# A decoder trunk on one core: the sum A21 + A22 of each Strassen pair made by an accumulating DMA, the other weight forms rebuilt from it, and the raw weights in four regions

## The chip, the core and the metric

The kernel runs on one NeuronCore of a Trainium2 chip. TensorE (PE in the profile) multiplies, VectorE (DVE) and ScalarE (ACT) do elementwise work, GpSimd (POOL) does a few small operations, and SyncE (SP) issues every DMA of the kernel before the change. The metric is the device time of one execution in microseconds. Three executions of the kernel before took 2245.98, 2249.03 and 2248.22 us; the median is 2248.22 us.

## The reference, cut to what matters

One decoding step of a small trunk of two layers, for 512 prompt tokens and 8 sample tokens, so 520 tokens in all, with 2048 channels:

```
for i in range(DEPTH):                                   # 2 layers
    h = rmsnorm(x, norm_g)
    z = h @ w_in                                         # [520, 2048] @ [2048, 8192]
    b_c, c_c, x_c, g_c, q, k, v, g_r = split_projection(z)
    y_conv = b_c * conv3(c_c * x_c) * silu(g_c)
    y_ret  = group_norm(retention(rope(q), rope(k), v)) * silu(g_r)
    x = x + concat(y_conv, y_ret) @ w_out                # [520, 2048] @ [2048, 2048]
    x = x + sigmoid(x @ w_pg) * (p[i] @ w_ple)           # [520, 2048] @ [2048, 2048]
y = rmsnorm(x, final_g)
```

All is float32. Nearly all arithmetic lies in the products with `w_in`, `w_out` and `w_pg`. The outputs also hold the new states of the convolution and of the retention, the latter 256 KB for each head and sample.

## The kernel before, in words

**Products.** The channels lie on the partitions. A weight matrix is cut into M tiles (128 output channels) and K tiles (128 input channels); the tokens are cut into two halves of 260. Each float32 operand is split into two float32r parts that add up exactly (`split`, `split_w`), and a product takes three matmuls of a 128x128 weight tile with 128x260 tokens (`mm3`, lines 216 to 218 of the profile): high by high, high by low, low by high.

**Strassen pairs.** Two neighbouring M tiles go together in `strassen`. Over the first `s` K tiles (a number from the tables `HEADS`, `CONVS`, `OUTS`, `GATES`, one for each pair) it forms seven products in place of eight; the weights of one pair are four blocks A11, A12, A21, A22 of `q = s // 2` K tiles each, and the products need A11, A12, A22 and the four forms A21+A22, A21+A22-A11, A11-A21, and A12 less the second of these. The other `KT - s` K tiles go by plain products at the end of the pair. The tables hold 89 Strassen pairs; 34 of them have `s = 14`, so q = 7. Over all pairs q adds up to 452.

**Weights.** `raws` (and `load`, for the plain K tiles) asks `raw_ring` for a place and issues the DMAs from SP (line 268, pieces of 2 or 3 K tiles; line 191, pieces of up to 4). The ring is 36 units of one weight tile; a request gets the neighbouring units that have been free for longest, at any start. `add` (line 275, DVE) makes the four forms in place, in pieces of up to 3 tiles. `split_w` (ACT line 198, DVE line 199) splits a piece into `split_ring`, a ring of 60 units, which holds the high and low parts of 30 tiles; the matmuls read there. A piece of `raw_ring` is free when its last split is done, and a piece of `split_ring` when its last matmul is done.

**Order.** A scheduling layer sets the order of each engine's instructions when the program is built, from priorities (weights have a raised one, `WPRIO`). The order on each engine, on each queue and on each ring is then fixed; SP, POOL, ACT and DVE wait in that order.

**Stages.** Each layer has: the retention heads (four groups of M tiles, with small matmuls for scores and states between the pairs, taken from the list `later` by `aside()`, and with the decode steps of the samples, `sample_step`, lines 579 to 587, which load a state and broadcast rows `kq` and store the new state `o_rets`); the convolution (8 groups of two pairs, mostly q = 7); the output projection; and the gate. In the profiled execution the heads run at about 50 to 450 us and 1130 to 1560 us, and the convolutions behind them.

**POOL** does only three sorts of work in the running part: a memset of `qks`, the powers -1/2 of the group norms (`rstp`, line 728) and those of the channel norms (`r5p`, line 456).

Of the kernel before, what the change touches and what calls it, by code (L numbers as in the profile page):

```python
# [13 lines left out]
P = 128  # L14
# [26 lines left out]
# How many K tiles go by Strassen in each pair of M tiles of the four products with weights.  # L41
# [13 lines left out]
def k_order(s):  # L55
    """The K tiles of a product whose first s go by Strassen: the first of each pair, the second, the rest."""
    return list(range(0, s, 2)) + list(range(1, s, 2)) + list(range(s, KT))


class Slots:  # L60
    """Equal on-chip slots of [128, 520] words, given out oldest-freed first."""
# [22 lines left out]
class Ring:  # L84
    """On-chip place for weights, in units of one tile; a request gets the neighbouring units freed longest ago."""

    def __init__(self, pool, n, dtype, name):
# [4 lines left out]

    def get(self, n):
        _, i = min((max(self.freed[i : i + n]), i) for i in range(len(self.freed) - n + 1))
# [6 lines left out]
    def fits(self, n):  # L101
        return min(max(self.freed[i : i + n]) for i in range(len(self.freed) - n + 1)) < BUSY
# [8 lines left out]
class Banks:  # L111
    """The accumulators of the products with weights, given out oldest-freed first."""
# [17 lines left out]
class Val:  # L130
    """A product's [128, 520] result: two accumulators, or a slot. Iterates as (tokens, view)."""
# [18 lines left out]
class Op:  # L150
    """A [128, 520] operand in two parts: a slot for each part, or a slot for each half of the tokens."""
# [13 lines left out]
def trunk_kernel(  # L165
# [17 lines left out]
    raw_ring = Ring(const, RAW, F32, "raw")  # L183
# [18 lines left out]
    def chunks(a, b, most=CH):  # L202
        """a to b in equal pieces: [(first, after last)]"""
# [10 lines left out]
    def mm3(out, wh, wl, xh, xl, start, stop, more=False):  # L214
        """more: the sum goes on after a stop and a read"""
# [6 lines left out]
    def product(out, w, c, xs, start, stop, more=False):  # L222
        """out (+)= sum over i of W[:, tile c + i]^T X[i], all in two parts"""
# [10 lines left out]
    def aside():  # L234
        """Work of the tensor engine that waits for a place between two products"""
        if later:
            later.pop(0)()

    def gemm(ops, src, s):
        """One M tile, all tokens; the K tiles lie in k_order(s)."""  # L240
# [10 lines left out]
    def strassen(ops, sums, src0, src1, s):  # L251
        """Two M tiles: Strassen's seven products in Winograd's form over the first s K tiles (halves of
        M, of K and of the tokens), the plain products over the others."""
# [949 lines left out]
```

## Time and profile before

| | |
|---|---|
| median of three executions | 2248.22 us |
| span of the profiled execution, first to last instruction | 2245.6 us |
| the difference of these two, which lies around the span | 2.6 us |
| DVE busy | 1837.1 us, 82% |
| ACT busy | 1290.3 us, 57% |
| POOL busy | 31.4 us, 38 instructions |
| HBM read, written | 294.70 MB, 43.58 MB |

The times of the profile come from one execution on the chip. A group's row gives the line of the source, the engine, the operation, the tiles written and read, the shapes, the count, then after the bar its busy time, the mean duration of one in ns, and the idle time of the engine just before these instructions with what ended most of it. Matmuls overlap, so their mean duration (284 ns) is longer than the time from one to the next.

### The profile page before, as it was taken

The page shows a single profiled execution, that of the slowest core. Times are in us where ns is not written, and L with a number is a line of the kernel's source. Part 1 is how long each engine was busy: PE and PEld are TensorE (multiplying, and loading weights), DVE is VectorE, ACT ScalarE, POOL GpSimd, SP SyncE. Part 2 cuts the span into 40 slices and gives each one's busy share as a digit, 9 for nine tenths or more (in the row PEclk, how much of TensorE's full clock was granted, in tenths as well). Part 3 has the DMA queues.
Part 4 walks back from the last instruction along what each step waited for, and adds up shares of the span by engine and source line. Part 5 has one row for each costly group of instructions (what it writes and reads, how often), then busy time and mean ns, then how long its engine had stood idle before and what let it go on. Part 6 is the DMA issues. An engine that isn't in the chain of part 4 may idle for free.

```text
span 2245.6 us, 50947 instructions
## 1 busy us (share of the span) xinstructions
PE 2219.0 (99%) x18364; PEld 2212.4 (99%) x18364; DVE 1837.1 (82%) x4363; ACT 1290.3 (57%) x3119; POOL 31.4 (1%) x38
## 2 busy tenths in 40 slices
PE   9999999999999999999999999999999999999998
PEld 8999999999999999999999999999999999999998
DVE  7787878788998888878786878787998888789785
ACT  6555555555655545655754455555565555556565
POOL 0000000000000000000000000000000000000000
PEclk9999999999999999999999999999999999999999
DMA  7445454644334645645743463546443345447445
GB/s 245 126 144 165 153 182 135 186 126 133 109 98 125 207 123 155 194 150 154 228 127 103 134 195 116 186 144 188 128 122 100 116 148 177 150 131 222 136 141 185
DMA packets 243582, 341.65 MB, mean 152 GB/s; under 512 B 28032, under 2 KB 153472, under 8 KB 243328
## 3 DMA queue, kind: packets, MB, share of 16 engines
q1 hardware_dynamic: 243328, 338.39, 49.0%
q8 instruction: 144, 2.36, 0.4%
q14 instruction: 110, 0.90, 0.1%
HBM read 294.70 MB, written 43.58 MB: 151 GB/s over the span
## 4 chain that ended last, share of the span: by engine, by line
PE 92%; DMA 5%; DVE 1%; ACT 1%; issue 1%; SPq 0%; DVEq 0%; POOL 0%; ACTq 0%
PE ps_g L216 28%; PE ps_g L217 28%; PE ps_g L218 28%; DMA slot<-kq 2%; DMA o_rets<-slot 1%; PE ps_p L216 1%; PE ps_p L217 1%; PE ps_p L218 1%; DMA slot<-x2s 1%; PE ps_s L216 0%; PE ps_s L218 0%; PE ps_s L217 0%; PE ps_o L218 0%; PE ps_o L217 0%; PE ps_o L216 0%
## 5 line engine op out<-in xcount | busy, mean ns | idle before, releaser
L216 PE MATMUL ps_g<-slot,split 128*128 128x260 f32 x5640 | 1577.1, 284 | 18.3 <-ACT slot L263 10.2
L217 PE MATMUL ps_g<-slot,split 128*128 128x260 f32 x5640 | 1585.7, 283 | 0.0
L218 PE MATMUL ps_g<-slot,split 128*128 128x260 f32 x5640 | 1572.4, 283 | 0.0
L198 ACT ACTIVATE split<-raw 128x256 fp32r<-128x256 f32 (+3 forms) x1738 | 797.8, 476 | 668.9 <-PE ps_g L217 341.8
L216 PEld LDWEIGHTS ps_g<-slot,split 128*128 128x128 f32 x5640 | 1057.0, 189 | 20.8 <-ACT slot L263 12.4
L217 PEld LDWEIGHTS ps_g<-slot,split 128*128 128x128 f32 x5640 | 1065.2, 189 | 0.3 <-DVE slot L377 0.2
L218 PEld LDWEIGHTS ps_g<-slot,split 128*128 128x128 f32 x5640 | 1057.5, 189 | 0.0
L199 DVE TENSOR_TENSOR split<-raw,split 128x256 fp32r<-128x256 f32 (+2 forms) x1738 | 827.6, 496 | 237.8 <-ACT split L198 121.2
L275 DVE TENSOR_TENSOR raw<-raw 128x256 f32<-128x256 f32 (+2 forms) x768 | 345.9, 465 | 10.3 <-DMA raw<-wo 3.3
L263 ACT ACTIVATE slot<-ps_g 128x260 f32<-128x260 f32 x445 | 167.8, 377 | 46.4 <-PE ps_g L218 43.3
L263 DVE TENSOR_TENSOR slot<-ps_g,slot 128x260 f32<-128x260 f32 x267 | 111.6, 421 | 18.8 <-PE ps_g L218 17.9
L376 ACT ACTIVATE slot<-slot 128x520 fp32r<-128x520 f32 (+1 forms) x189 | 104.9, 583 | 38.1 <-DVE slot L355 8.7
L377 DVE TENSOR_TENSOR slot<-slot,slot 128x520 fp32r<-128x520 f32 (+1 forms) x189 | 115.7, 631 | 5.8 <-ACT slot L376 5.3
L582 ACT ACTIVATE slot<-slot,vs 128x256 f32<-128x256 f32 x128 | 58.3, 502 | 97.8 <-DMA slot<-kq 74.5
L542 DVE TENSOR_TENSOR slot<-slot,slot 128x520 f32<-128x520 f32 x142 | 95.5, 692 | 6.1 <-PE ps_o L218 5.9
L583 DVE SCALAR_TENSOR_TENSOR slot<-slot,vec,slot 128x512 f32<-128x512 f32 x64 | 47.8, 749 | 54.3 <-ACT slot L582 47.1
L587 DVE CUSTOM_DVE_ANT_0 slot<-slot,slot 128x256 f32<-128x256 f32 x128 | 49.3, 418 | 0.1
L263 DVE TENSOR_TENSOR slot<-slot 128x260 f32<-128x260 f32 x89 | 37.5, 421 | 0.1
L216 PE MATMUL ps_p<-slot,split 128*128 128x260 f32 (+1 forms) x124 | 35.0, 282 | 0.0
L217 PE MATMUL ps_p<-slot,split 128*128 128x260 f32 (+1 forms) x124 | 34.9, 282 | 0.0
L218 PE MATMUL ps_p<-slot,split 128*128 128x260 f32 (+1 forms) x124 | 34.9, 281 | 0.0
L440 DVE TENSOR_TENSOR slot<-slot,slot 128x520 f32<-128x520 f32 x43 | 29.8, 694 | 4.4 <-ACT slot L439 4.4
(172 smaller groups left out, 1216.1 us busy)
## 6 DMA issues: line engine op xcount, KB each, us to landing
raw<-wi SPq DMA_DIRECT2D x268, 192.0 KB
raw<-wi SPq DMA_DIRECT2D x388, 128.0 KB
raw<-wi SPq DMA_DIRECT2D x117, 256.0 KB
slot<-kq SPq DMA_DIRECT2D x64, 256.0 KB
slot<-sret SPq DMA_DIRECT2D x64, 256.0 KB
o_rets<-slot SPq DMA_DIRECT2D x64, 256.0 KB
slot<-x1s SPq DMA_DIRECT2D x60, 260.0 KB
slot<-x2s SPq DMA_DIRECT2D x54, 260.0 KB
```

The costliest lines, as they stand in the source:

```text
L198: S.activation(hi, raw, AF.Copy)
L199: V.tensor_tensor(lo, raw, F(hi), SUB)
L216: PE.matmul(out, wh, xh, start=start, stop=False, skip_group_check=more)
L217: PE.matmul(out, wh, xl, start=False, stop=False, skip_group_check=more)
L218: PE.matmul(out, wl, xh, start=False, stop=stop, skip_group_check=more)
L263: fn(*args)
L275: V.tensor_tensor(out[:, n], x[:, n], y[:, n], op)
L376: S.activation(hi, src[:, n], AF.Copy)
L377: V.tensor_tensor(lo, src[:, n], F(hi), SUB)
L542: V.tensor_tensor(out[:, n], v, table[:, n], MUL)
L582: S.activation(kv[:, 256 * e : 256 * e + 256], kb[:, 256:512], AF.Identity, scale=vs[:, h, e, b : b + 1])
L587: V.tensor_tensor_reduce(kv[:, c], st[:, c], kb[:, :256], 1.0, 0.0, MUL, ADD, osum[:, e, h, b : b + 1])
```

## The change

It does four things.

1. In `strassen`, A21 is loaded by SP as before, and then POOL issues DMAs that read A22 from HBM and add it to A21 in its place (`G.dma_start(..., accum_op=ADD)`, line 300 of the new file), one for each piece of 2 or 3 K tiles. The place then holds A21 + A22. A22 is still loaded by itself as well, now asked for before the first product instead of behind it.
2. The other forms are rebuilt from it with three adds in place of four: A11 - (A21 + A22), then A11 - A21 as that plus A22, then A12 plus that first form. The first of these has the other sign than the form it replaces, and so `operand_sums` makes its second sum with the other sign; its fourth keeps its value.
3. `raw_ring` gets a step: a request of more than 4 units may start only at the units 0, 8, 16 and 24, a smaller one at every fourth unit.
4. In the products' order, the place that held A11 now carries the third and sixth product and the one that held A21 the fifth; which place is given back first changes with it.

```diff
-    def __init__(self, pool, n, dtype, name):
+    def __init__(self, pool, n, dtype, name, step=0):
+        self.step = step
...
+    def starts(self, n):
+
+        return range(0, len(self.freed) - n + 1, (self.step if n > 4 else 4) if self.step else 1)
+
     def get(self, n):
-        _, i = min((max(self.freed[i : i + n]), i) for i in range(len(self.freed) - n + 1))
+        _, i = min((max(self.freed[i : i + n]), i) for i in self.starts(n))
...
-    raw_ring = Ring(const, RAW, F32, "raw")
+    raw_ring = Ring(const, RAW, F32, "raw", 8)
...
         w11 = raws(src0, 0)
+        w21 = raws(src1, 0)
+        for i, j in chunks(0, q, CHL):
+            G.dma_start(w21[:, P * i : P * j], src1[:, P * (q + i) : P * (q + j)], accum_op=ADD)
+        w22 = raws(src1, q)
         times(a, w11, k1, True, False)
         copy(z0[:, LEFT], a)
-        w21, w22 = raws(src1, 0), raws(src1, q)
         add(w11, w11, w21, SUB)
-        add(w21, w21, w22, ADD)
         times(b, w21, t1, True, False)
         copy(z1[:, RIGHT], b)
-        add(w21, w22, w11, SUB)
-        times(a, w21, t2, False, True)
+        add(w21, w11, w22, ADD)
+        times(a, w11, t2, False, True)
         copy(z0[:, RIGHT], a)
         w12 = raws(src0, q)
-        add(w21, w12, w21, SUB)
+        add(w11, w12, w11, ADD)
         times(d, w12, at(ops, k2, LEFT), True, False)
         raw_ring.put(w12)
         aside()
-        times(a, w11, t3, False, True)
-        raw_ring.put(w11)
+        times(a, w21, t3, False, True)
+        raw_ring.put(w21)
...
-        times(b, w21, at(ops, k2, RIGHT), False, True)
-        raw_ring.put(w21)
+        times(b, w11, at(ops, k2, RIGHT), False, True)
+        raw_ring.put(w11)
...
-        V.tensor_tensor(t12[:, RIGHT], f1[:, RIGHT], t12[:, LEFT], SUB)
+        V.tensor_tensor(t12[:, RIGHT], t12[:, LEFT], f1[:, RIGHT], SUB)
         V.tensor_tensor(t34[:, LEFT], f1[:, RIGHT], f0[:, RIGHT], SUB)
-        V.tensor_tensor(t34[:, RIGHT], f1[:, LEFT], t12[:, RIGHT], SUB)
+        V.tensor_tensor(t34[:, RIGHT], f1[:, LEFT], t12[:, RIGHT], ADD)
```

The rest of the diff takes out comments, which moves line numbers: 191, 198, 199, 268 and 275 become 196, 203, 204, 273 and 280, and 456, 622 and 728 become 464, 630 and 736.

Three places show what moves. The first is POOL in the first head of layer 0, before and after (`rstp` is the power of the group norm, `raw` the raw weights, `wi` the packed `w_in`):

```order
L456 TENSOR_TENSOR r5p<-r_596,half_neg 128x5
L622 MEMSET qks 128x128
L728 TENSOR_TENSOR rstp<-rstd,half_neg 128x2 x2
L622 MEMSET qks 128x128
```

```order
L464 TENSOR_TENSOR r5p<-r_596,half_neg 128x5
L300 DMA raw<-wi 128x256
L630 MEMSET qks 128x128
L300 DMA raw<-wi 128x384
L300 DMA raw<-wi 128x256 x2
L736 TENSOR_TENSOR rstp<-rstd,half_neg 128x2 x2
L300 DMA raw<-wi 128x256 x3
```

The powers now stand in line with DMAs that wait for loads; over the program POOL gets 192 such DMAs.

The second is SP at a q = 7 pair in the middle of the convolutions of layer 0, the one whose weights are loaded from 566 us on, before and after. A block of 7 K tiles is three DMAs (2, 2 and 3 tiles), so a pair's blocks read 256, 256, 384, and the two K tiles left over are the two DMAs of line 191 (196):

```order
L268 DMA raw<-wi 128x256 x2
L268 DMA raw<-wi 128x384
L268 DMA raw<-wi 128x256 x2
L268 DMA raw<-wi 128x384
L268 DMA raw<-wi 128x256 x2
L268 DMA raw<-wi 128x384
L268 DMA raw<-wi 128x256 x2
L268 DMA raw<-wi 128x384
L191 DMA raw<-wi 128x256 x2
```

```order
L273 DMA raw<-wi 128x256
L273 DMA raw<-wi 128x384
L273 DMA raw<-wi 128x256 x2
L273 DMA raw<-wi 128x384
L273 DMA raw<-wi 128x256 x2
L273 DMA raw<-wi 128x384
L273 DMA raw<-wi 128x256 x2
L273 DMA raw<-wi 128x384
L273 DMA raw<-wi 128x256
L196 DMA raw<-wi 128x256 x2
```

Before, the blocks come as A11, A21, A22, A12. After, the second and third piece of A12 come first, then A11, A21, A22, and A12's first piece last, since a leftover K tile of the pair ahead lies in that piece's units; each piece of A21 is issued two DMAs later.

The third is DVE at the same pair, before and after (line 199/204 the split, 275/280 the adds, 263/268 the sums of results):

```order
L275 TENSOR_TENSOR raw<-raw 128x256 x4
L199 TENSOR_TENSOR split<-raw,split 128x384
L275 TENSOR_TENSOR raw<-raw 128x384
L199 TENSOR_TENSOR split<-raw,split 128x256
L275 TENSOR_TENSOR raw<-raw 128x384
L199 TENSOR_TENSOR split<-raw,split 128x256
L275 TENSOR_TENSOR raw<-raw 128x256
L263 TENSOR_TENSOR slot_447_7546<-slot_447_7546 128x260
```

```order
L280 TENSOR_TENSOR raw<-raw 128x256
L204 TENSOR_TENSOR split<-raw,split 128x256
L280 TENSOR_TENSOR raw<-raw 128x256
L204 TENSOR_TENSOR split<-raw,split 128x384
L280 TENSOR_TENSOR raw<-raw 128x384
L204 TENSOR_TENSOR split<-raw,split 128x256 x2
L280 TENSOR_TENSOR raw<-raw 128x256
L268 TENSOR_TENSOR slot_447_7546<-slot_447_7546 128x260
```

Before, the first six adds make A11 - A21 and A21 + A22; after, the first three make A11 less the sum that the DMAs have made, and the three of the sum are gone.

More of the change, by code (lines that the diff above doesn't have):

```diff
@@ L101, in fits @@
     def fits(self, n):
-        return min(max(self.freed[i : i + n]) for i in range(len(self.freed) - n + 1)) < BUSY
+        return min(max(self.freed[i : i + n]) for i in self.starts(n)) < BUSY
     def put(self, *parts):
```

## The prediction

> **What bounds the kernel now.** I read the page's first part, then its groups, then PE's idle time, then the stretches of the program.
>
> ```profile
> PE 2219.0 (99%) x18364; PEld 2212.4 (99%) x18364; DVE 1837.1 (82%) x4363; ACT 1290.3 (57%) x3119; POOL 31.4 (1%) x38
> L216 PE MATMUL ps_g<-slot,split 128*128 128x260 f32 x5640 | 1577.1, 284 | 18.3 <-ACT slot L263 10.2
> L198 ACT ACTIVATE split<-raw 128x256 fp32r<-128x256 f32 (+3 forms) x1738 | 797.8, 476 | 668.9 <-PE ps_g L217 341.8
> L275 DVE TENSOR_TENSOR raw<-raw 128x256 f32<-128x256 f32 (+2 forms) x768 | 345.9, 465 | 10.3 <-DMA raw<-wo 3.3
> ```
>
> PE is busy for 2219.0 us of a span of 2245.6 us: 18364 matmuls at 2219.0 / 18364 = 0.121 us from one to the next. The change adds and drops no matmul, so all that it could save is the 26.6 us in which PE is idle. Of these the row of line 216 names 18.3 us of waits. ACT's row says the same from the other side: the splits wait for PE to free their ring (341.8 us behind line 217 alone), so weights are normally ready ahead of need. The next view, waits of PE, tells what the 18.3 us are:
>
> ```profile
> PE ps_g L216 <- ACT slot L263: 10.2, 8, 2.4
> PE ps_g L216 <- ACT slot L379: 5.5, 1, 5.5
> PE ps_g L216 <- ACT split L198: 1.5, 1, 1.5
> ```
>
> 5.5 us is the start, before any weight; the change does not touch it. 10.2 us in 8 waits is PE waiting for ACT to copy an accumulator. Only 1.5 us is a late split. Sums by stretch (length; busy PE, PEld, DVE, ACT, POOL; clock; DMA share; GB/s) show where:
>
> ```profile
> 50.00:450.00 400.00, 396.33 (x3270) 393.91 (x3270) 316.57 (x805) 216.53 (x534) 7.25 (x12) 1.00 0.50 155
> 450.00:750.00 300.00, 300.00 (x2507) 300.00 (x2506) 258.17 (x637) 172.10 (x443) 5.43 (x1) 1.00 0.42 125
> 1130.00:1560.00 430.00, 420.32 (x3425) 417.37 (x3426) 338.34 (x834) 230.10 (x552) 8.43 (x11) 0.99 0.47 144
> 1560.00:1860.00 300.00, 300.00 (x2509) 300.00 (x2508) 264.80 (x642) 174.61 (x435) 5.87 (x1) 1.00 0.43 129
> ```
>
> The convolutions (second and fourth row), where most pairs have q = 7 and DVE is fullest (258 of 300 us), have no idle PE at all. The heads (first and third) have 3.7 and 9.7 us. The chain of waits just ahead of the longest of these stops, and of one more, reads (start, us, what):
>
> ```profile
> 1226.45 5.23 DMA o_retp<-slot
> ...
> 1231.74 4.16 DMA slot<-kq
> ...
> 1235.93 0.91 ACT slot L582 x2
> 1236.83 0.28 ACT slot L263
> ```
> ```profile
> 1432.07 6.07 DMA slot<-kq
> ...
> 1441.38 5.47 DMA o_rets<-slot
> ```
>
> A decode step's DMA of 256 KB takes 4 to 6 us, ACT stands at it in order (line 582), and the copy that PE needs (line 263) stands behind. So the kernel is PE-bound throughout, and its few stops come from DMA latency through ACT, not from DVE.
>
> **The change, part by part. DVE's adds.** Three adds stay of four, so 768 / 4 = 192 go. At the group's mean that is 192 x 0.465 = 89 us of DVE, 4% of the span. In the convolutions it can save nothing: PE has no idle there. In the heads it shortens the way to a kq load only where that load stands behind a DVE split in SP's queue. I take -1 us, with bounds of 0 and -9: half of the 18.3 us, since the other half is the start's 5.5 us and the landings themselves.
>
> **The accumulating DMAs.** 192 of them read the 452 K tiles of A22 once more: 452 x 64 KiB = 29.6 MB on top of 341.65 MB moved. They lengthen one chain: load of A21, POOL, accumulate, split, product. No row shows an accumulating DMA, and none a DMA issued by POOL. Nearest rows, of the chain of waits and of two tiles on POOL:
>
> ```profile
> 431.74 3.01 DMA slot<-xT
> ```
> ```profile
> 328.29 3.60 DMA raw<-wi
> 1115.51 5.24 DMA raw<-wi
> ```
> ```profile
> L728 POOL TENSOR_TENSOR rstp<-rstd,half_neg x16: 695/698/1070, 110.3 to 1533.8; 128x2 f32<-128x2 f32 x16
> ```
> ```profile
> L456 POOL TENSOR_TENSOR r5p<-r,half_neg x3: 850/1177/1957, 44.0 to 2226.1; 128x5 f32<-128x5 f32 x2, 128x3 f32<-128x3 f32 x1
> ```
>
> Lower bound: the shortest plain transfer, 3.0 us, issue included. Upper bound: POOL's slowest small operation and two of the slowest transfers one after the other, since the sum's place has to be read and written back: 2.0 + 2 x 6.07 = 14.1 us. I take a middling POOL operation and a usual load, 1.2 + 3.6 = 4.8 us, the value nearest to the rows of the same tile.
>
> Does 4.8 us fit? Take the pair that the order shows. A21's first piece is issued where A22's was, two DMAs later, so at the 570.66 below; the split of the finished sum stood at 579.00:
>
> ```profile
> 570.66 0.33 SPq L268 DMA_DIRECT2D raw<-wi  x1
> ```
> ```profile
> 579.00 0.42 ACT L198 ACTIVATE split<-raw 128x256 fp32r<-128x256 f32 x1 [0.57 <-PE ps_g L217]
> ```
>
> That is 8.3 us; less a load of 3.6 us, 4.7 us are left. So at 4.8 us the sum is just in time for the same split, which itself waited for PE ("<-PE ps_g L217") and so was not late. Behind it stands the stock: 60 units hold 30 tiles in two parts, 30 x 3 x 0.121 = 10.9 us of matmuls at most. Counted along the waits of the changed order, 119 matmuls stand between the one whose end lets that load go and the first that cannot run without its sum: 119 x 0.121 = 14.4 us. Off that go a split on DVE (0.42), SP's issue (0.33), a load (3.6) and ACT's split and copy (0.42 + 0.38): 9.2 us are left for an accumulate. The tightest chains of all, in the heads, have 80 and 83 matmuls (9.7 and 10.0 us), which leave 4.5 and 4.9 us. Cost at 4.8 us: 0.3 us. The cover is this stock; without it, each us over 9.2 costs a us in each of 34 pairs.
>
> [...]
>
> **The engines that move the data.** The queue row and the waits of SP's queue:
>
> ```profile
> q1 hardware_dynamic: 243328, 338.39, 49.0%
> ```
> ```profile
> SPq L268 <- DVE split L199: 576.2, 380, 10.5
> SPq L580 <- PE ps_o L217: 15.9, 6, 3.3
> ```
>
> 338.39 MB take 49.0% of 16 engines; 29.6 MB, counted twice because the place is read too, is 59 / 338 x 49 = 8.6 points more. I take 5% longer landings, 0.25 us on 5 us, for the 8 waits of the heads: +2 us, with bounds of 0 and +12 (1.5 us on each of 8).
>
> **Four regions.** A q = 7 block used to take exactly 7 units anywhere; now it starts at 0, 8, 16 or 24, and a leftover piece of 1 to 3 tiles closes a whole region until it is split. Loads that go later: in the order of before, past the start, none has fewer than 16 us between the matmul that frees its place and the one that needs its own product; after, 17 have, the two least of them, at about 1367 and 1465 us, 6.2 and 7.9 us (matmuls times 0.121). A plain load needs 0.42 + 0.33 + 3.6 + 0.42 + 0.42 = 5.2 us of that with the DVE split. With a landing of 5.24 us it is 6.8, and both are in the heads, where ACT also stands at kq loads. SP waits for a place most of its time (576.2 us in 380 waits), so a late place holds back what is queued behind it, kq loads (line 580) included. I take +2 us, bounds 0 and +8 (2 us at each of the four least).
>
> **POOL's queue.** The powers (16 of `rstp`, 0.70 us each) now stand behind accumulating DMAs that wait for loads. Behind `rstp` come ACT's normalisation, the transposes of the gate and, in SP's queue, `o_retp` and a kq load, as in the chain at 1226 us. Counted along the waits, the matmuls between what `rstp` needs and what needs it stay 6.5 us or more as before; a POOL issue of 1 us ahead of it fits. Cost 0, bounds 0 and +4 (one us at four of them).
>
> **Signs of the token sums, changed order of the places.** Same instructions, same shapes: 0.
>
> The sum: 2245.6 - 1 + 0.3 + 2 + 2 = 2248.9 us of span; with the 2.6 us that lie around it, 2251.5 us against 2248.22: I predict **2251 us**.
>
> **The rivals.**
>
> *Faster through DVE.* If the kq stops were partly DVE's (the split that SP waits for comes later even when DVE is 78% busy), 89 us less of it would halve PE's 18.3 us: 2248.22 - 9 = 2239; with the +2 of the regions 2241 us. For it: SP's 576.2 us behind DVE splits. Against it: chains ahead of the stops are DMA for 4 to 6 us each, DVE for less than 1.
>
> *Slower through a long accumulate.* One mechanism: the piece of A21 becomes a sum later than the stock lasts, in each q = 7 pair. It decides from 9.2 us on; at 10.5 us it costs 34 x 1.3 = 44 us: 2295 us; at the upper bound 34 x 4.9 = 167 us. For it: nothing in the trace shows such a DMA. Against it: no single transfer in the chain takes over 6.07 us.
>
> *Slower through slower landings.* If an accumulate keeps the engines busy several times longer than a plain load of its size, every landing grows by 1.5 us: +12 us on the heads' 8 waits and as much again where loads with little time come late: 2248 + 24 less what DVE gives, some 2270 us. For it: 4 to 6 us landings at a share of 0.47 to 0.50. Against it: at the start, at a share of 0.81, PE is idle 5.5 of 50 us, which is its wait for the first operand and nothing else.
>
> ```profile
> 0.00:50.00 50.00, 44.47 (x343) 43.99 (x344) 36.02 (x69) 37.81 (x81) 2.07 (x10) 1.00 0.81 269
> ```
>
> *POOL shut out by DVE.* If POOL could prepare a DMA only while DVE rests (42 of 300 us in the first convolutions), one us of preparation would take 300 / 42 = 7 us, the accumulate 3.6 + 8.2 = 11.8 us: 34 x 2.6 = +88 us, 2340 us. [...] I give it little.
>
> **How the numbers follow.** Chances: forecast 0.55 (2244 to 2258), faster through DVE 0.18, slower landings 0.15, long accumulate 0.08, POOL shut out 0.04. A measurement of this kernel tells a change of about 0.2%, 4.5 us, from none: under 2243.7 is faster, over 2252.7 slower. Faster: 0.15 of the DVE case and 0.02 of the forecast, 0.17. Slower: 0.27 of the three slow cases and 0.12 of the forecast's upper part, 0.39. Same: 0.44. The range 2242 to 2275 leaves out half of the DVE case (0.09) and the two slowest cases (0.12).
>
> **What would show it.** PE busy within 3 us of 2219.0 and no idle PE in the convolutions show that the accumulate is covered; idle PE there in every pair, behind line 203, shows the long accumulate. DVE near 1750 us with PE's waits on ACT's line 268 unchanged at 8 to 14 us shows that DVE was not the limit; waits halved show the first rival. Landings of kq in the chain at 4 to 6 us show that the engines cope; 6 to 8 us the slower landings. A row on POOL for line 300 of over 2 us, or some rows far longer than others, shows POOL shut out. New waits of PE for a split near 1367 or 1465 us show the regions. I am wrong if the accumulate holds the ring's places so long that SP's queue stops as a whole, which no row here prices.

## The result, and the profile after

| | before | after |
|---|---|---|
| median of four executions | 2247.1 us | 2338.59 us (2326.15 to 2339.94) |
| ratio, 95% interval | | 1.040 (1.038 to 1.0419) |
| span of the profiled execution | 2245.6 us | 2335.5 us |
| PE busy, PE idle in the span | 2219.0 us, 26.6 us | 2248.4 us, 87.1 us |

The changed kernel is 4% slower, some 90 us, where 2251 us and at most 2275 us had been predicted. The span grew by 89.9 us: 60.5 us are idle PE, 29.4 us more busy PE. The page's first part and its groups, of the changed kernel:

```profile
PE 2248.4 (96%) x18364; PEld 2230.6 (96%) x18364; DVE 1750.3 (75%) x4171; ACT 1266.8 (54%) x3119; POOL 201.4 (9%) x230
L221 PE MATMUL ps_g<-slot,split 128*128 128x260 f32 x5640 | 1596.0, 286 | 78.5 <-ACT slot L268 70.1
L203 ACT ACTIVATE split<-raw 128x256 fp32r<-128x256 f32 (+3 forms) x1738 | 777.5, 474 | 705.0 <-PE ps_g L222 257.8
L280 DVE TENSOR_TENSOR raw<-raw 128x256 f32<-128x256 f32 (+2 forms) x576 | 262.9, 468 | 207.2 <-DMA raw<-wi 132.1
```

DVE became 87 us shorter, as the adds that went away promised, and nothing came of it. DVE now stands idle for 207.2 us ahead of the adds that remain (line 280), where the group of before had 10.3 us. PE's waits for ACT to copy an accumulator (line 268) went from 10.2 to 70.1 us. The waits, by engine and line (us in total, times, longest), tell what ACT and DVE wait for:

```profile
PE ps_g L221 <- ACT slot L268: 70.1, 44, 4.3
DVE raw L280 <- DMA raw<-wi: 132.1, 62, 5.7
DVE raw L280 <- DMA raw<-wo: 47.7, 18, 5.6
DVE raw L280 <- DMA raw<-wg: 23.3, 11, 4.3
ACT split L203 <- DMA raw<-wi: 107.0, 54, 7.0
ACT split L203 <- DVE raw L280: 95.9, 66, 6.8
ACT slot L590 <- DMA slot<-kq: 79.5, 41, 4.7
```

The kq waits of the decode steps hardly moved (74.5 us before), and ACT's waits for DVE's adds fell (132.3 us before). What grew are the waits of DVE's add and of ACT's split for a transfer of weights: before, ACT's split waited 6.5 us in all for `wi`, and DVE's adds 3.3 us for `wo`. Sums by stretch, of the changed kernel (heads and convolutions of layer 0, its projection and gate, then the same of layer 1):

```profile
50.00:450.00 400.00, 392.05 (x3205) 389.21 (x3205) 301.68 (x765) 212.67 (x520) 29.41 (x38) 0.99 0.56 162
450.00:850.00 400.00, 394.00 (x3263) 391.56 (x3263) 311.37 (x755) 211.47 (x554) 45.51 (x47) 1.00 0.55 147
850.00:1150.00 300.00, 287.33 (x2339) 285.19 (x2339) 225.16 (x506) 175.73 (x420) 19.98 (x23) 0.98 0.59 171
1150.00:1580.00 430.00, 418.38 (x3380) 414.39 (x3379) 317.55 (x775) 223.90 (x538) 35.95 (x40) 0.98 0.53 154
1580.00:1880.00 300.00, 282.08 (x2314) 279.03 (x2313) 229.34 (x565) 156.94 (x404) 31.65 (x37) 0.99 0.51 136
1880.00:2335.00 455.00, 429.98 (x3525) 427.16 (x3524) 328.30 (x738) 248.32 (x605) 35.78 (x36) 0.98 0.57 168
```

and of the kernel before, the two stretches of projections and gates, which the prediction did not show:

```profile
850.00:1130.00 280.00, 279.46 (x2330) 279.03 (x2328) 232.03 (x517) 177.90 (x414) 0.00 (x0) 1.00 0.57 177
1860.00:2245.00 385.00, 378.42 (x3158) 378.12 (x3156) 306.94 (x679) 226.16 (x541) 2.33 (x3) 0.99 0.52 162
```

Length less PE's busy time is idle PE. The heads had 13.4 us (3.7 + 9.7) and now have 19.6; the convolutions had none and have 23.9 (6.0 + 17.9); projections and gates had 7.1 (0.5 + 6.6) and have 37.7 (12.7 + 25.0). So the cost is not in the convolutions alone, and least in the heads, where PE already waited.

**One late sum, step by step.** The timeline of the changed kernel at the pair that the prediction used, start and duration of each group of instructions (in brackets the idle time ahead of it and what ended it):

```profile
576.98 0.37 ACT L268 ACTIVATE slot<-ps_g 128x260 f32<-128x260 f32 x1
580.42 0.20 ACT L818 ACTIVATE ncv<-slot 128x2 f32<-128x2 f32 x1 [3.07 <-DVE slot L550]
...
581.25 1.12 ACT L203 ACTIVATE split<-raw 128x256 fp32r<-128x256 f32 x3
...
582.19 0.89 DVE L204 TENSOR_TENSOR split<-raw,split 128x256 fp32r<-128x256 f32 x2
...
584.40 0.86 POOL L300 DMA_DIRECT2D raw<-wi  x1 [18.60 <-DMA raw<-wi]
585.66 1.75 POOL L300 DMA_DIRECT2D raw<-wi  x2 [0.40 <-issue]
...
588.86 0.43 DVE L280 TENSOR_TENSOR raw<-raw 128x256 f32<-128x256 f32 x1 [2.23 <-DMA raw<-wi]
...
591.32 0.43 DVE L280 TENSOR_TENSOR raw<-raw 128x256 f32<-128x256 f32 x1 [1.70 <-DMA raw<-wi]
...
591.33 0.42 ACT L203 ACTIVATE split<-raw 128x256 fp32r<-128x256 f32 x1 [2.04 <-DMA raw<-wi]
591.65 0.37 ACT L268 ACTIVATE slot<-ps_g 128x260 f32<-128x260 f32 x1
...
592.07 0.39 PE L221 MATMUL ps_g<-slot,split 128*128 128x260 f32 x1 [1.14 <-ACT slot L268]
```

Follow the second piece of A21. The matmul that lets its place be emptied ends at 577.5. But ACT stands in order at line 818, the convolution's elementwise work, and waits there 3.07 us for DVE; so the split that empties the place starts on ACT at 581.25 and on DVE at 582.19. SP issues the load at 582.63, it lands at 585.13; POOL's accumulate is issued at 585.66 and lands at 591.22. 13.7 us have gone by since the matmul. In the same 0.1 us DVE's add and ACT's split start, which had waited for it; ACT's copy of an accumulator stands behind that split, and PE, which waits for that copy, starts 0.4 us after it has started, having been idle for 1.14 us. PE does not wait for a weight, then: it waits for a copy that is queued behind a split that waits for a sum. DVE itself was behind at that time: it had waited 3.3 us in all for three sums of the pair ahead (stops that ended at 567.17, 569.40 and 570.89 us), and then worked without a pause until 581.2 us.

**The busy time.** Part of the 29.4 us more of busy PE is a lower clock. In the trace's clock records the granted clock falls to 0.5 in 12 stretches ahead of the end (3 before), 10 of 3.41 us and 2 of 6.83 us. Two pieces beside each other in the changed kernel, behind a stop of 3.09 us that ended at 965.0:

```profile
966.00:969.00 3.00, 3.00 (x15) 3.00 (x15) 3.00 (x7) 1.81 (x3) 0.00 (x0) 0.50 0.38 112
969.00:972.00 3.00, 3.00 (x27) 3.00 (x26) 2.09 (x5) 0.81 (x3) 0.00 (x0) 0.99 0.47 138
```

15 matmuls in 3 us against 27. From one matmul's start to the next, 382 intervals in the run lie between 0.20 and 0.26 us, 199 more than before; at 0.10 us more than the usual 0.12 each, that is 20 us. Most of the rest of the busy time is the last matmul of each stop, which shows at its full 0.28 us: start-to-start gaps of over 0.4 us were 15, and are 60.

### The profile page after: what moved, and what is told of

The parts are those of the page before. It is cut to its first block, busy times and chain, and to the rows that moved or that the text cites. A ratio compares the mean times of both kernels' runs of the same rounds, so it can differ in the third digit from the quotient of the medians.

```text
span 2335.5 us, 51521 instructions
## 1 busy us (share of the span) xinstructions
PE 2248.4 (96%) x18364; PEld 2230.6 (96%) x18364; DVE 1750.3 (75%) x4171; ACT 1266.8 (54%) x3119; POOL 201.4 (9%) x230
## 3 DMA queue, kind: packets, MB, share of 16 engines
q0 software_dynamic: 27648, 29.63, 8.3%
## 5 line engine op out<-in xcount | busy, mean ns | idle before, releaser
L221 PE MATMUL ps_g<-slot,split 128*128 128x260 f32 x5640 | 1596.0, 286 | 78.5 <-ACT slot L268 70.1
L203 ACT ACTIVATE split<-raw 128x256 fp32r<-128x256 f32 (+3 forms) x1738 | 777.5, 474 | 705.0 <-PE ps_g L222 257.8
L204 DVE TENSOR_TENSOR split<-raw,split 128x256 fp32r<-128x256 f32 (+2 forms) x1738 | 816.8, 498 | 211.5 <-ACT split L203 135.1
L280 DVE TENSOR_TENSOR raw<-raw 128x256 f32<-128x256 f32 (+2 forms) x576 | 262.9, 468 | 207.2 <-DMA raw<-wi 132.1
L300 POOL DMA_DIRECT2D raw<-wi x132 | 115.5, 943 | 1215.6 <-DMA raw<-wi 872.7
L385 DVE TENSOR_TENSOR slot<-slot,slot 128x520 fp32r<-128x520 f32 (+1 forms) x189 | 116.5, 635 | 10.3 <-ACT slot L384 10.2
L550 DVE TENSOR_TENSOR slot<-slot,slot 128x520 f32<-128x520 f32 x142 | 95.9, 694 | 6.1 <-PE ps_o L223 5.8
L300 POOL DMA_DIRECT2D raw<-wo x32 | 28.0, 982 | 289.8 <-DMA raw<-wo 245.2
L300 POOL DMA_DIRECT2D raw<-wg x28 | 24.3, 897 | 332.9 <-DMA raw<-wg 213.4
L268 DVE TENSOR_TENSOR slot<-slot 128x260 f32<-128x260 f32 x89 | 37.7, 423 | 2.8 <-ACT slot L268 2.8
L576 ACT ACTIVATE slot<-slot 128x520 f32<-128x520 f32 x32 | 20.2, 634 | 30.2 <-DVE slot L550 30.2
```

Source lines behind the costliest of these rows:

```text
L203: S.activation(hi, raw, AF.Copy)
L204: V.tensor_tensor(lo, raw, F(hi), SUB)
L221: PE.matmul(out, wh, xh, start=start, stop=False, skip_group_check=more)
L268: fn(*args)
L280: V.tensor_tensor(out[:, n], x[:, n], y[:, n], op)
L300: G.dma_start(w21[:, P * i : P * j], src1[:, P * (q + i) : P * (q + j)], accum_op=ADD)
```

## The experiments

Two theories go through the expectations. **L**: the sum is late. Its chain (a matmul frees the place, split, load, accumulate, then add and split in the order of DVE and ACT) is longer than the matmuls that stand beside it. **R**: the rest of the change does it, the four regions above all. Every time below is a median beside the kernel before on the same chip, every ratio is to that kernel, with its 95% interval.

### Which part of the change costs

`no_pool` and `pool_plain` edit the accumulating DMA:

```diff
-        for i, j in chunks(0, q, CHL):
-            G.dma_start(w21[...], src1[...], accum_op=ADD)      # no_pool
...
-            G.dma_start(w21[...], src1[...], accum_op=ADD)      # pool_plain
+            G.dma_start(w21[...], src1[...])
```

`dve_sum` is no_pool with one add more, and `regions_only` is the kernel before with the two lines of the ring:

```diff
+        add(w21, w21, w22, ADD)                                 # dve_sum, behind copy(z0[:, LEFT], a)
...
-    raw_ring = Ring(const, RAW, F32, "raw")                     # regions_only, with the class Ring of after
+    raw_ring = Ring(const, RAW, F32, "raw", 8)
```

> The changed kernel without its 192 accumulating DMAs: A21 stands where A21 + A22 should, which part of the computation is left out; the four regions, the three adds and the order of requests stay. Theory L (the loop: a place freed by a DVE split, load of A21, accumulate, the add on DVE that waits for it in order; DVE idles about 4 us in each q = 7 pair): the stops of PE go, 2245 us +- 6, PE's waits on ACT's copy back at 8 to 14 us, and clock at 0.5 in 3 to 5 stretches. Theory R (the regions give places late): stays over 2300. Theory T (more bytes keep the DMA engines busy, all landings later): also 2245, so this run does not tell L from T.

> The same 192 DMAs from POOL behind the load of A21, but plain: A22 overwrites A21, so A21 is left out of the sum. Theory L (it is the second transfer in line that costs, whatever it does): 2315 to 2345 us, POOL DMA to landing 3.5 to 4.5 us in place of 4.9. Theory C (adding in the DMA engines is what costs): landing under 3 us and under 2280 us.

> The kernel before with the four regions alone; adds, forms and request order of before. Theory R: over 2300 us. Theory L: the regions cost what late places cost by themselves, 2247 to 2260 us, no stop of PE in the q = 7 stretches.

> The changed kernel with the sum A21 + A22 made by a fourth add on DVE, no DMA from POOL; regions, forms and early request of A22 stay. Theory L: 2245 to 2262 us: all but the accumulate is harmless. Theory R: over 2300 us. A time over 2262 with DVE above 81% would say that the order of requests costs as well.

| | time | ratio |
|---|---|---|
| no_pool | 2247.79 us | 1.0008 (0.9993 to 1.0022) |
| pool_plain | 2275.07 us | 1.0142 (1.0109 to 1.0174) |
| regions_only | 2249.67 us | 1.0011 (0.9999 to 1.0023) |
| dve_sum | 2251.99 us | 1.0024 (1.0012 to 1.0037) |

Without the accumulating DMAs all other parts of the change together cost nothing that can be measured, and less work for DVE brings nothing: no_pool has both the regions and 1771.6 us of DVE, 66 us less than before. R falls. By the first line of its page PE is as busy as before:

```profile
PE 2214.7 (99%) x18364; PEld 2207.3 (98%) x18364; DVE 1771.6 (79%) x4171; ACT 1289.2 (57%) x3119; POOL 34.4 (2%) x38
```

A second transfer in line, even a plain one, costs 1.4%, some 32 us; that it accumulates costs 2.6% more, some 58 us. Neither expectation for pool_plain came true: L had 2315 us or more, and C, whose time it is (under 2280 us), had a landing under 3 us. What differs between these two is told by POOL's and the queue's rows, here of pool_plain:

```profile
L300 POOL DMA_DIRECT2D raw<-wi x132: 536/536/719, 44.8 to 1845.7; - x132
q0 software_dynamic: 10304, 29.63, 4.2%
raw<-wi POOLq DMA_DIRECT2D x86, 128.0 KB, 3.3
raw<-wi POOLq DMA_DIRECT2D x46, 192.0 KB, 3.9
```

and here of the changed kernel (min/median/max ns of one; packets, MB, share of 16 engines; KB and median us from issue to landing):

```profile
L300 POOL DMA_DIRECT2D raw<-wi x132: 862/865/1538, 44.7 to 1896.4; - x132
q0 software_dynamic: 27648, 29.63, 8.3%
raw<-wi POOLq DMA_DIRECT2D x86, 128.0 KB, 4.8
raw<-wi POOLq DMA_DIRECT2D x46, 192.0 KB, 5.1
```

For the same 29.63 MB an accumulate takes 0.33 us more of POOL, 2.7 times the packets, twice the engines' time and, in these rows of `wi`, 1.2 to 1.5 us more from issue to landing. Whether the 58 us come from the longer chain or from the doubled traffic these runs did not tell.

### Traffic or lateness

`acc_aside` keeps the traffic and takes it out of the chain; `spare` is a tile of four units that nobody reads, and a small POOL operation that reads two words of A21 makes each accumulate wait for the load of A21 as before:

```diff
+            o = 2 * P * (i == 2 and j == 4)
+            G.tensor_tensor(spare[:, o : o + 2], w21[:, P * i : P * i + 2], w21[:, P * i : P * i + 2], ADD)
-            G.dma_start(w21[:, P * i : P * j], src1[...], accum_op=ADD)
+            G.dma_start(spare[:, o : o + P * (j - i)], src1[...], accum_op=ADD)
```

The three others keep the chain and start it earlier, or need its end later. "Lead" in the expectations is counted in the built order: the matmuls between the last one on which the transfer depends and the first that depends on it, times 0.1195 us.

```diff
+        w21 = raws(src1, 0)          # sum_first: A21 and its accumulate ahead of A11
+        ... G.dma_start(w21[...], src1[...], accum_op=ADD)
         w11 = raws(src0, 0)
...
         copy(z0[:, LEFT], a)
+        w12 = raws(src0, q)          # d_first: the product with A12 second
+        times(d, w12, at(ops, k2, LEFT), True, False)
         add(w11, w11, w21, SUB)
...
-        w12 = raws(src0, q)
         add(w11, w12, w11, ADD)
-        times(d, w12, at(ops, k2, LEFT), True, False)
```

> The 192 accumulating DMAs keep their size, source and place in line, but add into a spare tile that nobody reads; POOL paces each by reading two words of the piece of A21 that SP has loaded (192 small POOL operations more). The weights then hold A21 in place of the sum. Theory L (the sum comes too late for its consumers): the traffic costs little, time 2248 to 2256 us, no stop of PE behind line 203 in the convolutions. Rival T (the accumulates' traffic and issue slow the engines for everybody): the 63 us between plain and accumulating transfers stay, 2300 us or more.

> A21 and its accumulate are asked for ahead of A11, so the sum's chain starts one place earlier: counted along the waits, the matmuls between what lets an accumulate's chain start and what needs it go from a median of 14.6 us to 16.6 us. Theory L: the chain was late by the 1.8 us that an accumulate takes more than a plain transfer, which cost 63 us, so 2.0 us more lead bring 50 to 75 of the 90 us back: 2262 to 2288 us. Rival T: same DMAs, same traffic, 2330 us or more. If SP's queue as a whole is the limit (places come free too late), no gain either.

> The product with A12 goes second, so the sum is needed one product later; median lead of the accumulate's chain 18.1 us against 14.6 us, that of SP's loads 14.5 us against 16.6 us. Theory L: 60 to 85 of the 90 us come back, 2252 to 2278 us. Rival T: 2330 us or more. If the shorter lead of the plain loads weighs as much, 2290 us or more with waits of ACT's split for plain loads of A11 or A12.

> Both: lead of the accumulate's chain 21.1 us in the median, of SP's loads 13.4 us. Theory L: the accumulate is covered, 2246 to 2262 us, and what is left comes from plain loads. Rival T: 2330 us or more.

| | time | ratio |
|---|---|---|
| acc_aside | 2251.06 us | 1.0021 (1.0012 to 1.0031) |
| sum_first | 2292.79 us | 1.0201 (1.0182 to 1.0220) |
| d_first | 2313.93 us | 1.0290 (1.0266 to 1.0315) |
| sum_d_first | 2277.96 us | 1.0138 (1.0118 to 1.0158) |

Of acc_aside, the waits of PE and the rows of POOL and of the queue:

```profile
PE ps_g L223 <- ACT slot L270: 12.0, 12, 2.7
L305 POOL DMA_DIRECT2D spare<-wi x132: 865/880/1056, 44.8 to 1827.3; - x132
q0 software_dynamic: 27648, 29.63, 8.6%
```

The packets are the same, POOL takes nearly the same time for each, and PE's waits are close to those of before (10.2 us there). So the traffic costs little, 0.2% with an interval to 0.3%, 7 us, and what costs is that the sum is late. One thing did not stay: in the spare tile an accumulate lands 4.0 us in the median after its issue, in the changed kernel 4.9. The other three go the way of L, but the sizes were missed: by the ratios sum_first brought 45 us of the 90 back (2262 to 2288 us were expected), d_first 25 (2252 to 2278 expected), both 59 (2246 to 2262 expected). Lead in the median is thus not the whole of it: d_first has the longer one, 18.1 us against 16.6, and costs more. Its expectation had named a second case, 2290 us or more if the shorter lead of the plain loads weighs as much, and its time lies there; the control d_first_dve below bears on that.

### More lead by a fifth region

`five` gives the raw ring 39 units, so five regions, and the split ring 59; two more kernels take the orders above as well:

```diff
-RAW, SPLIT = 36, 60
+RAW, SPLIT = 39, 59
```

`d_first_dve`, `five_sum_first_dve` and `sum_d_first_dve` are the controls: the same orders with the accumulating DMAs taken out and `add(w21, w21, w22, ADD)` put ahead of the first add, as in dve_sum.

> Raw ring of 39 units, so five regions (starts 0 to 32) in place of four; the split ring gives one unit (59). Order of the requests as in the changed kernel. Counted along the waits the median lead of the accumulate's chain goes from 14.6 to 16.4 us, that of SP's loads from 16.6 to 18.0 us. Theory L: at the lead of sum_first (16.6 us) it costs as much or less, 2255 to 2292 us. Rival S (what is short is the lead of the plain loads, SP's queue as a whole): since that is as long as before the change, the cost goes altogether, 2250 us or less. Rival O (sum_first gained through its order, not through lead): 2330 us or more.

> Five regions and A21 asked for first: median lead of the accumulate's chain 18.8 us, its 5% point 14.4 us (11.95 in the changed kernel), SP's loads 17.7 us. Theory L: 2246 to 2262 us, DVE's waits at line 280 for transfers under 40 us in all, PE's behind ACT's line 268 under 25 us. If the cost is not one of lead: 2280 us or more.

> Five regions, A21 first and the product with A12 second: median lead of the accumulate's chain 20.7 us, 5% point 16.3 us, SP's loads 15.5 us. Theory L: 2244 to 2256 us, level with the kernel before. If the order with A12 second costs by itself, 2262 us or more, and then d_first_dve shows the same cost without an accumulate.

> d_first with the sum made by DVE's fourth add and no accumulating DMA: lead of SP's loads 13.3 us in the median, 623 of 1686 under 12 us. It prices d_first's order alone. Theory L: plain loads are covered at this lead, 2248 to 2258 us, so nearly all of d_first's 68 us and of sum_d_first's 30 us comes from the accumulate. Rival S: 2270 us or more.

> five_sum_first with the sum made by a fourth DVE add and no accumulating DMA. If the 31 us of five_sum_first are the accumulate's: 2246 to 2258 us. If they belong to the order with A21 first and the five regions: 2266 us or more.

> sum_d_first with the sum made by a fourth DVE add. d_first_dve cost 10 us, so the order is not free: 2254 to 2264 us, which leaves 15 to 25 of the 31 us of sum_d_first to the accumulate. 2270 us or more would lay all of them on the order.

| | time | ratio |
|---|---|---|
| five | 2291.30 us | 1.0199 (1.0183 to 1.0215) |
| five_sum_first | 2276.50 us | 1.0137 (1.0120 to 1.0154) |
| five_sum_d_first | 2283.72 us | 1.0174 (1.0156 to 1.0192) |
| d_first_dve | 2256.29 us | 1.0047 (1.0032 to 1.0062) |
| five_sum_first_dve | 2253.34 us | 1.0040 (1.0030 to 1.0050) |
| sum_d_first_dve | 2263.01 us | 1.0086 (1.0067 to 1.0106) |

five costs what sum_first costs, at the same lead (16.4 and 16.6 us) by another way; so it is the lead and not the order that helps. Rival S had laid the cost on the plain loads and expected 2250 us or less, since their median lead goes from 16.6 to 18.0 us in five; it is out. No_pool says so too: it has the plain loads and their order, and costs nothing. But five_sum_first and five_sum_d_first missed their expectations by 14 and 28 us: the cost does not go to nothing at 19 us. The controls show why in part. The orders are not free, and in the four cases below, each with a control, what the accumulate costs more than a DVE add falls with its lead:

| accumulate in | median lead | ratio less that of its control | us |
|---|---|---|---|
| the changed kernel (control dve_sum) | 14.6 us | 0.0376 | 85 |
| d_first | 18.1 us | 0.0243 | 55 |
| five_sum_first | 18.8 us | 0.0097 | 22 |
| sum_d_first | 21.1 us | 0.0052 | 12 |

The differences carry the intervals of two ratios, some 5 us each way. Five_sum_d_first, at 20.7 us, has no control; its 1.0174 includes the cost of its order.

The median still is a poor measure, for 0.7 us of it part d_first from five_sum_first, and 33 us of cost. The traces and the built order give a better one: how many of the 192 sums land with less than 3 us of their lead left (the lead less the time from the matmul's end to the landing; the leads of this count come out some 0.4 to 1 us longer than those above). They are 83 in the changed kernel, 51 in d_first, 35 in sum_first, 33 in five, 8 in five_sum_first and 5 each in sum_d_first and five_sum_d_first. This puts d_first behind sum_first, where its time is. It is an order and not a price: pool_plain has 38 and costs 1.4%.

In five_sum_first the first convolutions are whole again, by the sums of its stretch:

```profile
450.00:850.00 400.00, 399.73 (x3337) 399.51 (x3336) 328.75 (x778) 223.64 (x571) 46.06 (x47) 1.00 0.54 149
```

0.3 us of idle PE stand where the changed kernel has 6.0. What remains are 20 waits of PE for a copy, 31.3 us in all, the longest in a q = 6 pair of the second. Its timeline there, and PE's longest wait:

```profile
1573.03 1.80 POOL L299 DMA_DIRECT2D raw<-wi  x2 [31.34 <-DVE slot L385]
...
1580.86 0.94 ACT L203 ACTIVATE split<-raw 128x384 fp32r<-128x384 f32 x2 [7.62 <-DMA raw<-wi]
...
1584.33 0.58 PE L221 MATMUL ps_g<-slot,split 128*128 128x260 f32 x1 [6.13 <-ACT slot L268]
```

SP had issued the pair's loads in one burst between 1566 and 1575 us, and the two accumulates landed 7.7 and 8.9 us after their issue, where the median is 4.8. So this stop came from two slow landings, not from a mean one. It was seen in one trace, not tried: no run took such bursts apart.

### Which pairs

`acc_q7` has accumulating DMAs only where q is 7 and a DVE add elsewhere, `acc_rest` the reverse, and `five_sum_first_q7` is five_sum_first with the first rule:

```diff
-        for i, j in chunks(0, q, CHL):
+        for i, j in chunks(0, q, CHL) if q == 7 else []:        # acc_rest: q < 7
...
+        if q < 7:                                               # acc_rest: q == 7
+            add(w21, w21, w22, ADD)
         add(w11, w11, w21, SUB)
```

> The changed kernel with accumulating DMAs only in the 34 pairs with q = 7 (102 DMAs); the 55 smaller pairs make the sum with a DVE add. The prediction's own reckoning laid the risk on the pairs with q = 7 alone: then nearly the whole 90 us stay, 2325 us or more. Theory M (any pair whose chain lacks the 14 to 15 us): median lead is 14.0 us here, so most, but not all, of the cost: 2295 to 2320 us.

> The other half: accumulating DMAs only in the 55 smaller pairs (90 DMAs, median lead 17.0 us, 33 of them under 16 us), DVE adds in the pairs with q = 7. If the cost is that of q = 7 alone: 2256 us or less. Theory M: a third of the chains is short, 2268 to 2295 us; and the two halves add up to about the 90 us, unless a late sum makes the next one late.

> Five regions, A21 first, accumulating DMAs only in the 34 pairs with q = 7 (4 of 102 chains under 14 us). If the 30 us that stayed in five_sum_first belong to the smaller pairs: 2247 to 2258 us. If they belong to bursts of loads in any stage, or to the order of the requests: 2268 us or more.

| | time | ratio |
|---|---|---|
| acc_q7 | 2310.18 us | 1.0267 (1.0228 to 1.0306) |
| acc_rest | 2278.25 us | 1.0135 (1.0109 to 1.0161) |
| five_sum_first_q7 | 2264.36 us | 1.0086 (1.0061 to 1.0112) |

The halves add up: 2.67% and 1.35% against 4.0%. Two thirds of the cost belong to the 34 pairs with q = 7 and a third, 30 us, to the 55 smaller ones; the prediction's whole term for a late sum was 0.3 us. five_sum_first_q7 fell between its two expectations and settles nothing on its own.

No version beat the kernel before, and none could be expected to: the kernel is bound by PE, and DVE's relief, which no_pool has without the accumulates, is worth nothing.

## Why the prediction was wrong, by its own steps

**What bounds the kernel: right.** PE does, and the convolutions had no idle time to give back.

**DVE's adds, -1 us with bounds of 0 and -9: right as far as the noise lets one see.** DVE has 87 us less to do, and no_pool is level with before (1.0008, 0.9993 to 1.0022).

**Duration of the accumulate, 4.8 us: right, in part by luck.** Over all 192 the landing took 4.89 us in the mean after POOL's issue began; the profile's medians for `wi` are 4.8 and 5.1 us. But the price had no term for the adding: it took 1.2 us for POOL and 3.6 us for a plain load, and POOL needed 0.87 us in the median (0.94 in the mean) and the rest 4.0 us, while the same transfer without the adding took 3.66 us in all. In the rows of 128 KB of `wi` the plain transfer from POOL took 3.3 us in the median and the accumulating one 4.8 us; the shortest of pool_plain's 192 took 2.4 us, the shortest accumulate 2.9.

**"Does 4.8 us fit?", cost 0.3 us: wrong, and this is the step that failed.** The right lead was counted, 119 matmuls or 14.4 us. But of what goes off, each instruction was priced by its own duration, as if each started when the one before it ended; and the result, a margin of 4.4 us, was worked out with one usual value for each step. Means over the transfers, from matching the built order to the trace:

```
us, mean                       prediction   before, 768   pool_plain, 192   after, 192   after, the 104 with
                                            plain loads                                  a lead under 16 us
matmul's end to DVE's split      0             0.98           1.35             1.80           2.08
the split on DVE                 0.42          0.50           0.49             0.49           0.47
to SP's issue                    0.33 (issue)  0.21           0.26             0.34           0.37
issue to landing                 3.6           3.04           3.26             3.32           3.38
landing to POOL's issue          -             -              0.62             0.59           0.61
POOL's issue to landing          4.8           -              3.66             4.89           4.96
matmul to landed sum             9.15          -              9.64            11.44          11.86
5% and 95% of that               -             -           6.5, 12.9        7.7, 15.3      8.1, 15.5
landed sum to the matmul         0.80          -              7.66             6.53           2.67
lead                            14.4           -             17.2             17.2           13.4
```

The instructions cost what was said; 2.7 us of waits between them were missing (2.08 us ahead of DVE's split, 0.61 ahead of POOL's issue), and 1.9 us more behind the sum, where ACT and DVE do other work first. In the 104 tightest chains that makes 11.86 + 2.67 = 14.5 us against 13.4 of lead: PE reaches the matmul in question a us later in the mean than its matmuls alone would take. The first of these waits could have been read: 0.98 us in the trace of before, with 5% of them over 3.37 us. And it is no constant. It grows from one run to the next as the sums get later, 0.98, 1.35 and 1.80 us. The likely reason is that a DVE and an ACT that stand waiting for one sum fall behind with the splits that free the next one's place; the pair at 577 us shows this once, and no run tried it by itself.

Nor is a mean what decides. Landed sums lie between 8.1 and 15.5 us, each pair waits for the latest of its pieces, and PE, which had no idle time, cannot win back what one piece loses. So the cost sets in well before mean and lead meet: pool_plain, whose chain is landed in 9.64 us, costs 32 us already. "It decides from 9.2 us on" was a step at a threshold; what the runs show is a slope, from 85 us at a lead of 14.6 us down to 12 at 21.1.

**Four regions, +2 us: nothing speaks against it** (regions_only 1.0011, 2.5 us, with an interval that holds 0 as well). **Slower landings, +2 us: nothing speaks against it.** The share of the queue came as 8.3 points, 8.6 had been said, and the loads landed in 3.32 us (of A21) in place of 3.04 us (of all blocks), 0.25 us more had been said; acc_aside's interval leaves the traffic 7 us at most. **POOL's queue, 0:** no run tried it alone; acc_aside, with the same DMAs ahead of the powers, leaves it no more than that.

**The rivals.** *Long accumulate* named the mechanism and its sign in the profile, idle PE in the convolutions, and gave it 0.08 and a condition that never came true: no accumulate took the 9.2 us from which it was to cost anything (4.89 us in the mean, 8.4 us the longest); the rest of the chain was longer than assumed. It also laid all risk on 34 pairs, and a third of the cost is elsewhere. *POOL shut out by DVE* gave 2340 us, next to what was measured, and was still wrong. No run shows the 7 us for one us of preparation that it was added up from: POOL's rows of line 300 take 0.862 us at least and 0.865 us in the median, and the median is also 0.865 over the 71 of the 192 accumulates in whose rows DVE was busy for 95% of the time or more. Of the 41 rows over 1.0 us (the longest took 1.57) 40 start before POOL's row ahead has ended. Its number came near by luck and is no support for its mechanism. *Faster through DVE* and *slower landings* are out by no_pool and acc_aside.

**What would have made it wrong** was named last: that the ring's places are held so long "that SP's queue stops as a whole, which no row here prices". That is near the loop that was found, but SP's queue did not stop: its waits behind DVE's splits went from 796.7 us (576.2 at line 268, 220.5 at line 191) to 914.3 us in a span that is 90 us longer. What the trace of before did price is the wait ahead of those splits, 0.98 us in the mean.

**What stays open.** The 12 to 22 us that an accumulate still costs at 19 to 21 us of lead are put down to its tail (the stop at 1584 us) by one place in one trace, and not by an experiment. Why five_sum_d_first costs more than five_sum_first at a longer lead was not tried either; with four regions its order alone cost 19 us (sum_d_first_dve). How the 85 us divide between waiting and the lower clock behind it was counted, some 20 us of it being clock, but no run held the clock.

## What to carry to other kernels

A transfer that is put between a load and its use lengthens a loop (place freed, load, transfer, use, place freed), and that loop must be summed with the time in each in-order queue ahead of its instructions, not with the instructions alone; the longest of those waits here, the one ahead of DVE's split, stands with 0.98 us in the trace before the change (2.08 us in the 104 tightest chains after it). Where the bounding engine is never idle, compare the loop's slow end, not its mean (here 15.5 and 11.86 us), with the lead, for it has no idle time from which lateness could be won back. Work taken from an engine that is 82% busy was worth nothing here, because of PE's stops before the change only one, of 0.9 us, waited for it.

## What had not been expected of the hardware

The 192 accumulating DMAs from POOL needed 27648 packets for their 29.63 MB where the plain ones of pool_plain needed 10304, each 0.865 us of POOL in place of 0.536, and all of them 8.3% of the engines in place of 4.2%; in a kernel whose engines are about half busy (49.0% in the queue row of before), all of that together cost some 0.2% (acc_aside) until the result was in a chain.

Short stops were followed by a lower clock. Of the 12 stretches at half clock in the changed kernel 11 follow a stop of 2.6 to 4.6 us, counted from one matmul's start to the next, and the three of the kernel before follow stops of 1.8, 2.1 and 2.7 us; a stop of 2.8 us at 1735 us in the changed kernel is followed by none. The stretches last 3.41 us or twice that. Length alone does not tell which stop is followed by one, since 1.8 us were enough in the kernel before and 2.8 us in the changed kernel were not. Where a stop falls tells more. The 12 stretches of the changed kernel all begin on one grid of 3.413 us, to 3 ns, and 11 of them follow a cell of this grid in which 12 matmuls or fewer started, where a full cell has 28 or 29; one follows a cell with 21. Behind the start, all cells at full clock with fewer than 12 were followed by half clock; of the two with 12 one was and one was not. The stop at 1735 us falls across two cells, which have 16 and 18. In the kernel before, the three stretches lie on a grid of the same step and follow cells with 14, 7 and 10, and another cell with 14, at 428 us, is followed by none; so these counts are no threshold, and no run tried what sets one.
